# The small half of every split weight: from a VectorE subtraction to an adding transfer onto a negated tile

## The chip, the cores and the metric

The kernel runs on one core of one Trainium2 chip. The metric is device time in microseconds (us) of one launch, median of three runs; lower is better.

## The reference, cut to what matters

The reference runs a transformer of three layers over 512 tokens of width 1024, all in float32: twice (feed-forward, mixer with two kinds of attention and a short convolution, feed-forward, per-layer embedding), then once (a mixer with pooling and a recurrence, feed-forward, per-layer embedding). What the change touches is every product of an activation with a weight matrix, such as

```
def swiglu(x, w_gate, w_up, w_down):
    return (jax.nn.silu(x @ w_gate) * (x @ w_up)) @ w_down
```

The kernel makes each such product in float32 accuracy out of three products of rounded halves: with W = Wh + Wl and h = hh + hl, it adds Wh·hh, Wh·hl and Wl·hh. Wh is W rounded to the shorter type fp32r that TensorE takes, and Wl is the remainder W − Wh, rounded too.

## The kernel before, in words

Features lie on the 128 partitions, the 512 tokens along the columns. A weight is cut into units, mostly 8 row blocks of 128 by 128 columns, that is 1024 columns in memory layout. One transfer on SyncE's queue brings one unit or a few small ones into a `raw` tile (four of them, `N_RAW`). `prep` then makes the unit's tiles of up to 512 columns: for each, a pair `wh`, `wl`. In all there are 993 pairs, 937 of them 512 columns wide. `wh` is a ScalarE copy of `raw` that rounds (L136). `wl` is a VectorE subtraction `raw` − `wh` (L137); it is not issued in `prep` but noted in `self.low` and issued by `flush_low`, just before the step's product for units that the step needs itself, else just after it. A tile of 512 columns feeds 4 row blocks, and each of these feeds three products (L273 with `wh` and `hh`, L274 with `wh` and `hl`, L275 with `wl` and `hh`).

`run` walks over a list of steps (a product, an emptying of its result, a part of a norm). Each engine executes its own instructions in the order in which this walk issues them. Before each step at most one further unit is prepared while fewer than `wu` units are alive: 8 in general, 6 in the attentions, 10 at the ends of sublayers. At a boundary between sublayers a table, PLAN, sets `wu` to 0 and later to 10, so that no weight is prepared while the norm and the residual are worked out.

At a boundary, ScalarE copies the broadcast norm factor `sb` out of PSUM (L511), VectorE updates the residual x (L526, L527) and makes `hl` (L516), ScalarE makes `hh` (L528), and GpSimd sums the squares (L619 for the old sublayer, L534 for the new one) and takes the power −0.5 (L311, `s`). In the latent attention GpSimd also moves 32 rows by transfers of its own queue (L1283, 64 KB each) and makes two remainders (L1291, L1292), while VectorE scales the probabilities `p` (L1327).

Of the kernel before, what the change touches and what calls it, by code (L numbers as in the profile page):

```python
# [5 lines left out]
F32 = mybir.dt.float32  # L6
# [3 lines left out]
AF = mybir.ActivationFunctionType  # L10
ALU = mybir.AluOpType
# [3 lines left out]
T = 512  # L15
# [12 lines left out]
# What is done after each of a boundary's products: 8 half sums of the ended sublayer's last tiles (second half of  # L28
# the tokens), then 8 steps over K of the next one's first products for each half of the tokens (A, B).
# e: tile out; ss, bc: the post-norm's sum and broadcast; a, b: residual; qss, qbc: sum and broadcast of the next  # L30
# norm; w: units of weights ahead. After an embedding its 8 projections come first; p: its first gates out.
# [26 lines left out]
class Unit:  # L58
    """a weight as the tensor engine takes it: [128 rows of K, dims], from the host array host(inputs)"""
# [7 lines left out]
class Raw:  # L67
    """units that one transfer brings"""
# [17 lines left out]
class Builder:  # L86
# [31 lines left out]
    def cols_units(self, w, k0, kn, c0, ncol, width=P):  # L118
        """units of the [K, N] matrix w(inputs): rows k0*128.., columns c0..c0+ncol, a unit of `width` columns each"""

        def host(inp, c):
            a = w(inp)[k0 * P : (k0 + kn) * P, c : c + width]
            return a.reshape(kn, P, width).transpose(1, 0, 2).reshape(P, kn * width)

        return [Unit(lambda inp, c=c: host(inp, c), (kn, width)) for c in range(c0, c0 + ncol, width)]

    def prep(self, u):
        """the unit's two parts: the first on ScalarE now, the rest of it on VectorE with flush_low"""
        kn, w = u.dims
        per = T // w  # L130
        u.tiles = []
        for k in range(0, kn, per):
            n = min(per, kn - k) * w
            h, l = self.a("wh", F32R)[:, 0:n], self.a("wl", F32R)[:, 0:n]
            src = u.raw.tile[:, u.at + k * w : u.at + k * w + n]
            self.S.copy(h, src)  # L136
            self.low.append((u, lambda h=h, l=l, src=src: self.V.tensor_sub(l, src, h.bitcast(F32))))  # L137
            u.tiles.append((h, l))
        u.hi = lambda k: u.tiles[k // per][0][:, (k % per) * w : (k % per + 1) * w]
        u.lo = lambda k: u.tiles[k // per][1][:, (k % per) * w : (k % per + 1) * w]  # L140

    def declare(self, raws):
        """the transfers' sources: arrays of up to 32 MB, each transfer's part contiguous"""
        i = 0
        while i < len(raws):
            j, n = i, 0
            while j < len(raws) and (j == i or n + raws[j].n <= 32 * 2048):
                raws[j].off = n * P
                n += raws[j].n
                j += 1  # L150
            part = raws[i:j]

            def host(inp, part=part, n=n):
                out = np.empty(n * P, np.float32)
                for r in part:
                    v = out[r.off : r.off + r.n * P].reshape(P, r.n)
                    for u in r.units:
                        v[:, u.at : u.at + u.n] = u.host(inp)
                return out

            ap = self.decl(f"w{i}", (n * P,), F32, host)
            for r in part:
                r.src = ap[r.off : r.off + r.n * P].rearrange("(p n) -> p n", p=P)
            i = j

# [14 lines left out]
    def hook(self, at, fns):  # L180
        """put each of fns after the next product from step `at` on"""
        i = at
        for fn in fns:
            while not self.steps[i][2]:
                i += 1
            self.steps.insert(i + 1, ([], fn, False) + self.steps[i][3:])
            i += 2

    def run(self):
        order, last = [], {}  # L190
# [34 lines left out]
        self.low = []  # L225

        def flush_low(us=None):
            keep = []
            for u, f in self.low:
                if us is None or u in us:  # L230
                    f()
                    u.raw.left -= 1
                    if u.raw.left == 0:
                        self.rlive -= 1
                else:
                    keep.append((u, f))
            self.low[:] = keep
            load_raws()

        def prep_next():  # L240
            u = order[self.uptr]
            if u.raw.tile is None:
                flush_low()
            assert u.raw.tile is not None
            self.prep(u)
            self.uptr += 1
            self.live += 1
# [5 lines left out]
        for i, (us, fn, _, wu) in enumerate(self.steps):  # L253
            need = max([pos[id(u)] for u in us], default=-1)
            n = 0
            while self.uptr <= need or (self.uptr < len(order) and self.live < wu and n < 1):
                prep_next()
                n += 1
            lat, self.later = self.later, []
            for f in lat:  # L260
                f()
            flush_low(us)
            fn()
            flush_low()
            for u in frees.get(i, ()):
                self.live -= 1
# [10 lines left out]
    def mmk(self, o, u, h, part, cols=slice(None), start=True, stop=True, ks=None, k0=0):  # L277
        """o[cols, tokens] (+)= W[:, cols]^T h"""
        ks = list(range(u.dims[0])) if ks is None else ks
        t0, t1 = part  # L280
        for i, k in enumerate(ks):
            hh, hl = h[k0 + k]
            self.mm3(o, u.hi(k)[:, cols], u.lo(k)[:, cols], hh[:, t0:t1], hl[:, t0:t1], start and i == 0, stop and i == len(ks) - 1)

    def mm_part(self, o, p, u, h, half=None):
        """o[p] = W^T h for the tokens p, or one half of the sum over K"""
        n = u.dims[0]
# [9 lines left out]
    def sums(self, acc, part):  # L297
        """for each token of the part, tokens on partitions: the sum of acc over its rows"""
# [7 lines left out]
    def rstd(self, v, part, mul, add, dst=None):  # L306
        """(v * mul + add) ** -0.5 for each token, tokens on partitions"""
# [6 lines left out]
    def bcast(self, s, part):  # L314
        """the tokens' values s along the columns, on all partitions"""
        o = self.ps("bc")
# [16 lines left out]
    def setup_late(self):  # L333
# [5 lines left out]
        # query on partitions, key on columns: keys after the query are masked  # L339
        G.affine_select(out=m[:, 0:P], in_=m[:, 0:P], compare_op=ALU.is_ge, fill=NEG, base=0, pattern=[[-1, P]], channel_multiplier=1)  # L340
        # key on partitions, query on columns: keys from the query on are masked
        G.affine_select(out=m[:, P : 2 * P], in_=m[:, P : 2 * P], compare_op=ALU.is_gt, fill=NEG, base=0, pattern=[[1, P]], channel_multiplier=-1)
        # -1 where row >= column
# [17 lines left out]
    def columns(self):  # L361
        """the per-feature vectors, a column of 128 for each tile of features"""
# [129 lines left out]
    def boundary(self, prev, nxt):  # L492
        """The last products of prev and the first of nxt go by token halves: while one half's norm and
        residual are worked out, the tensor engine has the other half's products."""
# [96 lines left out]
    def plain_head(self, sub, units, evac, evac_at="rb"):  # L591
        """four products of h, K outermost; each half of the tokens has its half of a bank, which evac(i, p, o)
        empties: once the norm is there ("rb"), or by halves of the tokens, the second later ("halves", "both")"""
# [16 lines left out]
    def final_sq(self, sub, src, p, last, first):  # L610
        """square of a result tile into the sublayer's sum"""
# [10 lines left out]
    def ffn(self, cols, pre, post, wg, wu, uoff, wd, pieces, pmul, padd, conv=None, nxt=None):  # L622
# [18 lines left out]
        def act_gate(n, p, og):  # L641
            """the gate of hidden tile n"""
# [112 lines left out]
    def proj_sub_tail(self, sub, units, rhs, begun={}):  # L755
        """the sublayer's last product: m-tiles in T layout, squares summed; begun[m] = [o, ks]: the part of
        tile m's sum that is there already"""
# [114 lines left out]
    def mix1(self, L, cols):  # L872
# [20 lines left out]
        def heads(name, kn, h0, h1, c0, c1):  # L893
            """columns c0..c1 of heads h0..h1 of a [kn * 128, heads * n] matrix"""
# [41 lines left out]
        def rank_ss(key):  # L936
            v = self.sums(st.acc[key], FULL)
            # the rank's rms is that of r * (h W): r^2 times the raw sum of squares
# [19 lines left out]
        def rotate(src, dh, dl):  # L958
            """src [128, 512] packed heads of 32 rows: rotated, as hi/lo"""
# [132 lines left out]
        def body():  # L1092
# [70 lines left out]
            # parts of the output product (tile, k) whose operands are there before the last heads  # L1163
# [32 lines left out]
    def mix1_heads(self, sub, st, L, fn):  # L1196
        V, S, G, E = self.V, self.S, self.G, self.E
        y_rows = fn["y_rows"]
        # where a block of 512 - 128 i columns (i = 0..3) lies in three tiles
# [184 lines left out]
    def mix2(self, cols):  # L1384
# [15 lines left out]
        def gate(g):  # L1400
            """two heads of 64 a tile, on the diagonal of a [128, 128] matrix"""
# [47 lines left out]
        def lam():  # L1449
            """c8 = -8 softplus(-lambda), by feature"""  # L1450
# [375 lines left out]
def _rope_const():  # L1826
    """per row of four packed heads of 32: inverse frequency, sign of the sine"""
# [24 lines left out]
```

## Time and profile before

| what | value |
|---|---|
| median of three runs | 2894.86 us (2893.38 to 2895.28) |
| profiled execution, span from the first to the last instruction | 2893.8 us |
| TensorE busy | 2861.5 us, 99% |
| VectorE busy | 1725.2 us, 60% |
| ScalarE busy | 1256.8 us, 43% |
| GpSimd busy | 340.1 us, 12% |
| DMA, 259.29 MB on SyncE's queue | 27.7% of 16 engines |

The profiled execution has no time of its own beside its span; the median of the runs is 1.1 us above that span. Busy times of TensorE are those of pipelined products, so 99% says that it nearly always has one in flight.

### The profile page before, as it was taken

The numbers are of one execution on the slowest core, as the hardware profiler recorded it, in microseconds if no ns is written. First come the engines' busy times: TensorE is split into PE (matmuls) and PEld (weight loads), VectorE is DVE, ScalarE is ACT, GpSimd is POOL, SyncE is SP. The second block draws the span as 40 slices with busy tenths as digits, with TensorE's granted clock in tenths as the row PEclk, the third lists the DMA queues.
The fourth block names the chain that finished last, engine by engine and source line by source line (L and its number), as shares of the span: only waits on it lengthen the run. The fifth ranks groups of instructions, "written<-read, shape, count | busy, mean of one in ns | idle before, by whom it ended". The sixth has DMA issues, their size and how long they took to land.

```text
span 2893.8 us, 38786 instructions
## 1 busy us (share of the span) xinstructions
PE 2861.5 (99%) x14926; PEld 2451.1 (85%) x14928; DVE 1725.2 (60%) x3033; ACT 1256.8 (43%) x2527; POOL 340.1 (12%) x385
## 2 busy tenths in 40 slices
PE   8999999999999999999999999999999999999999
PEld 7888888898888988888888888888988889888888
DVE  6464476965434695434658773444888746635458
ACT  5332346753322363322456653323656635433234
POOL 0000130430000240000312220000320003000013
PEclk9999999999999999999999999999999999999999
DMA  5323321223223223322222223233222332322320
GB/s 177 117 92 101 102 67 48 59 74 112 99 97 108 73 74 117 102 95 95 68 76 82 65 74 116 88 103 109 78 70 91 102 102 85 111 96 95 110 95 30
DMA packets 77608, 264.31 MB, mean 91 GB/s; under 512 B 9072, under 2 KB 10992, under 8 KB 77424
## 3 DMA queue, kind: packets, MB, share of 16 engines
q1 hardware_dynamic: 75456, 259.29, 27.7%
q0 software_dynamic: 1536, 2.10, 0.3%
q8 instruction: 117, 1.92, 0.3%
q14 instruction: 67, 0.55, 0.1%
q10 hardware_dynamic: 432, 0.45, 0.0%
HBM read 257.61 MB, written 2.10 MB: 90 GB/s over the span
## 4 chain that ended last, share of the span: by engine, by line
PE 83%; DVE 11%; ACT 3%; issue 1%; POOL 1%; DMA 0%; SPq 0%; DVEq 0%; ACTq 0%; POOLq 0%
PE gu L275 13%; PE gu L274 13%; PE gu L273 13%; PE pt L275 8%; PE pt L274 8%; PE pt L273 8%; PE in L273 3%; PE in L274 3%; PE in L275 3%; DVE x L527 2%; DVE hl L516 2%; DVE t L526 2%; PE hd L274 1%; DVE wl L137 1%; PE hd L275 1%
## 5 line engine op out<-in xcount | busy, mean ns | idle before, releaser
L137 DVE TENSOR_TENSOR wl<-raw,wh 128x512 fp32r<-128x512 f32 (+1 forms) x993 | 651.2, 700 | 144.8 <-ACT wh L136 141.3
L273 PE MATMUL gu<-hh,wh 128*128 128x512 f32 x1632 | 636.5, 390 | 0.0
L275 PE MATMUL gu<-hh,wl 128*128 128x512 f32 x1632 | 635.7, 390 | 0.0
L274 PE MATMUL gu<-hl,wh 128*128 128x512 f32 x1632 | 635.7, 390 | 0.0
L136 ACT CAST wh<-raw 128x512 fp32r<-128x512 f32 (+1 forms) x993 | 543.9, 605 | 177.6 <-PE pt L274 93.7
L273 PE MATMUL pt<-dh,wh 128*128 128x512 f32 (+1 forms) x1056 | 378.1, 358 | 0.0
L275 PE MATMUL pt<-dh,wl 128*128 128x512 f32 (+1 forms) x1056 | 377.3, 357 | 0.0
L274 PE MATMUL pt<-dl,wh 128*128 128x512 f32 (+1 forms) x1056 | 377.3, 357 | 0.0
L275 PEld LDWEIGHTS gu<-hh,wl 128*128 128x128 f32 x1632 | 306.5, 188 | 63.4
L274 PEld LDWEIGHTS gu<-hl,wh 128*128 128x128 f32 x1632 | 306.5, 188 | 63.3
L273 PEld LDWEIGHTS gu<-hh,wh 128*128 128x128 f32 x1632 | 306.5, 188 | 63.1
L619 POOL TENSOR_TENSOR acc<-acc,sq 128x256 f32<-128x256 f32 (+1 forms) x96 | 98.5, 1026 | 1880.5 <-ACT sq L617 1879.6
L294 ACT CAST dh<-ur 128x512 fp32r<-128x512 f32 x112 | 69.5, 621 | 470.1 <-DVE ur L676 464.2
L670 DVE TENSOR_TENSOR ur<-gu,rb 128x512 f32<-128x512 f32 x102 | 70.5, 691 | 264.6 <-PE gu L275 264.6
L274 PEld LDWEIGHTS pt<-dl,wh 128*128 128x128 f32 x1056 | 199.7, 189 | 28.9
L273 PEld LDWEIGHTS pt<-dh,wh 128*128 128x128 f32 x1056 | 199.7, 189 | 28.8
L275 PEld LDWEIGHTS pt<-dh,wl 128*128 128x128 f32 x1056 | 199.6, 189 | 28.5
L274 PE MATMUL hd<-hl,wh 128*128 128x256 f32 (+1 forms) x672 | 203.8, 303 | 5.7 <-DVE hl L516 4.8
L273 PE MATMUL hd<-hh,wh 128*128 128x256 f32 (+1 forms) x672 | 198.7, 296 | 6.9 <-ACT hh L451 6.9
L738 DVE TENSOR_TENSOR f<-pt,f 128x512 f32<-128x512 f32 (+1 forms) x100 | 58.2, 582 | 233.2 <-PE pt L275 233.1
L275 PE MATMUL hd<-hh,wl 128*128 128x256 f32 (+1 forms) x672 | 195.1, 290 | 0.5 <-DVE wl L137 0.5
L273 PE MATMUL in<-hh,wh 128*128 128x512 f32 x432 | 170.0, 394 | 0.0
(394 smaller groups left out, 4724.4 us busy)
## 6 DMA issues: line engine op xcount, KB each, us to landing
raw<-in_w_dram SPq DMA_DIRECT2D x450, 512.0 KB, 3.5
raw<-in_w_dram SPq DMA_DIRECT2D x36, 384.0 KB, 3.1
x<-in_x_dram SPq DMA_DIRECT2D x8, 256.0 KB, 5.9
raw<-in_w_dram SPq DMA_DIRECT2D x4, 432.0 KB, 3.7
pt<-in_p_dram SPq DMA_DIRECT2D x6, 256.0 KB, 4.0
out_dram<-pgt SPq DMA_DIRECT2D x10, 128.0 KB, 1.7
qh<-qrh POOLq DMA_DIRECT2D x16, 64.0 KB, 2.0
ql<-qrl POOLq DMA_DIRECT2D x16, 64.0 KB, 2.0
```

What stands on the lines that cost most here:

```text
L136: self.S.copy(h, src)
L137: self.low.append((u, lambda h=h, l=l, src=src: self.V.tensor_sub(l, src, h.bitcast(F32))))
L273: self.E.matmul(o, lh, rh, start=start, stop=False, **kw)
L274: self.E.matmul(o, lh, rl, start=False, stop=False, **kw)
L275: self.E.matmul(o, ll, rh, start=False, stop=stop, **kw)
L294: self.S.copy(hi, src)
L516: V.scalar_tensor_tensor(hl[:, t0:t1], x, nxt.gpre(m), hh[:, t0:t1].bitcast(F32), op0=ALU.mult, op1=ALU.subtract)
L526: V.scalar_tensor_tensor(t[:, t0:t1], prev.f[m][:, t0:t1], prev.gpost(m), st.sbt[:, t0:t1], op0=ALU.mult, op1=ALU.mult)
L527: V.tensor_add(x, x, t[:, t0:t1])
L619: eng.tensor_tensor(sub.acc[:, t0:t1], sub.acc[:, t0:t1], sq[:, t0:t1], op=ALU.add)
L670: V.tensor_mul(ur[:, t0:t1], ou, sub.rb[:, t0:t1])
L738: V.tensor_tensor(f, q, f, op=ALU.add)
```

## The change

For each tile, ScalarE writes a second tile right behind the rounding copy: `wl` = −`wh`. Then a transfer on GpSimd's queue reads the same 512 columns of W from memory a second time and adds them onto `wl`. VectorE's subtraction and the list `self.low` go. A `raw` tile now counts as free when ScalarE's copies of it have been issued. Comments and docstrings went too, so that line numbers are 10 or 11 lower further down: L137 is now the copy, L138 the negation and L139 the transfer.

```diff
     def prep(self, u):
...
             src = u.raw.tile[:, u.at + k * w : u.at + k * w + n]
             self.S.copy(h, src)
-            self.low.append((u, lambda h=h, l=l, src=src: self.V.tensor_sub(l, src, h.bitcast(F32))))
+            self.S.activation(l, h.bitcast(F32), AF.Copy, scale=-1.0)
+            self.G.dma_start(l, u.raw.src[:, u.at + k * w : u.at + k * w + n], accum_op=ALU.add)
             u.tiles.append((h, l))
+            u.raw.left -= 1
+            if u.raw.left == 0:
+                self.rlive -= 1
...
-        self.low = []
-
-        def flush_low(us=None):
-            keep = []
-            for u, f in self.low:
-                if us is None or u in us:
-                    f()
-                    u.raw.left -= 1
-                    if u.raw.left == 0:
-                        self.rlive -= 1
-                else:
-                    keep.append((u, f))
-            self.low[:] = keep
-            load_raws()
...
-                flush_low()
+                load_raws()
...
-            flush_low(us)
             fn()
-            flush_low()
+            load_raws()
```

The order on ScalarE at the very start of the program, before (the first weight's two tiles, then the first normed activations `hh`):

```order
L136 CAST wh_126<-raw_102 128x512
L136 CAST wh_129<-raw_102 128x512
L451 ACTIVATE hh_132<-x_104,cols 128x512
L451 ACTIVATE hh_136<-x_105,cols 128x512
L451 ACTIVATE hh_148<-x_106,cols 128x512
```

and in the changed kernel:

```order
L137 CAST wh_126<-raw_102 128x512
L138 ACTIVATE wl_127<-wh_126 128x512
L137 CAST wh_131<-raw_102 128x512
L138 ACTIVATE wl_132<-wh_131 128x512
L440 ACTIVATE hh_136<-x_104,cols 128x512
L440 ACTIVATE hh_140<-x_105,cols 128x512
```

Two negations now stand ahead of the first `hh`.

ScalarE at the end of the first per-layer embedding, before (two units of weights, then `sb`, the broadcast norm factor that the residual waits for):

```order
L136 CAST wh_9828<-raw_9591 128x512
L136 CAST wh_9831<-raw_9591 128x512
L136 CAST wh_9863<-raw_9605 128x512
L136 CAST wh_9866<-raw_9605 128x512
L511 COPY sb_9819<-bc_9886 128x256
```

and in the changed kernel:

```order
L137 CAST wh_10194<-raw_9951 128x512
L138 ACTIVATE wl_10195<-wh_10194 128x512
L137 CAST wh_10199<-raw_9951 128x512
L138 ACTIVATE wl_10200<-wh_10199 128x512
L137 CAST wh_10231<-raw_9967 128x512
L138 ACTIVATE wl_10232<-wh_10231 128x512
L137 CAST wh_10236<-raw_9967 128x512
L138 ACTIVATE wl_10237<-wh_10236 128x512
L500 COPY sb_10185<-bc_10256 128x256
```

Four negations have come between the copies and `sb`.

GpSimd in the first latent attention, in the changed kernel (L1272 are the 64 KB moves of rows, L1280 and L1281 the remainders `kl` and `ql` of one head's operands); before, the same rows stood there without the six L139:

```order
L1272 DMA qh_4859<-qrh_4342 32x512
L1272 DMA ql_4860<-qrl_4343 32x512
L139 DMA wl_4894<-in_w_dram 128x512
L139 DMA wl_4899<-in_w_dram 128x512
L1272 DMA qh_4861<-qrh_4342 32x512
L1272 DMA ql_4862<-qrl_4343 32x512
L1280 TENSOR_TENSOR kl_4866<-kn_4782,kh_4865 64x512
L1281 TENSOR_TENSOR ql_4862<-qn_4855,qh_4861 64x512
L139 DMA wl_5006<-in_w_dram 128x512
L139 DMA wl_5011<-in_w_dram 128x512
L139 DMA wl_5042<-in_w_dram 128x512
L139 DMA wl_5047<-in_w_dram 128x512
```

The weights' transfers stand among the heads' own work on one queue. Each of them waits for its negation on ScalarE, and for the completion of the transfer eight places ahead of it on that queue.

## Rows read from the trace of the kernel before

**Rows 1.** The page: span, busy times of the engines, shares of the last-ending chain.

```profile
span 2893.8 us, 38786 instructions
PE 2861.5 (99%) x14926; PEld 2451.1 (85%) x14928; DVE 1725.2 (60%) x3033; ACT 1256.8 (43%) x2527; POOL 340.1 (12%) x385
...
PE 83%; DVE 11%; ACT 3%; issue 1%; POOL 1%; DMA 0%; SPq 0%; DVEq 0%; ACTq 0%; POOLq 0%
PE gu L275 13%; PE gu L274 13%; PE gu L273 13%; PE pt L275 8%; PE pt L274 8%; PE pt L273 8%; PE in L273 3%; PE in L274 3%; PE in L275 3%; DVE x L527 2%; DVE hl L516 2%; DVE t L526 2%; PE hd L274 1%; DVE wl L137 1%; PE hd L275 1%
```

**Rows 2.** Stretches: PE, PEld, DVE, ACT, POOL busy (instructions), clock, DMA share, GB/s.

```profile
0.00:50.00 50.00, 42.43 (x174) 33.87 (x175) 27.71 (x62) 26.81 (x45) 2.09 (x7) 1.00 0.57 193
200.00:250.00 50.00, 50.00 (x223) 41.42 (x221) 17.85 (x29) 14.03 (x25) 0.00 (x0) 1.00 0.31 97
520.00:545.00 25.00, 23.01 (x118) 18.30 (x117) 24.54 (x51) 18.40 (x46) 13.98 (x14) 0.89 0.33 101
1035.00:1085.00 50.00, 46.44 (x363) 44.02 (x361) 45.93 (x90) 31.49 (x79) 21.75 (x26) 1.00 0.17 58
2850.00:2894.00 44.00, 38.63 (x250) 34.69 (x248) 39.08 (x76) 16.89 (x37) 14.89 (x14) 0.97 0.13 48
```

**Rows 3.** Groups of instructions by line: count, busy us, mean ns, idle before.

```profile
L137 DVE TENSOR_TENSOR wl<-raw,wh 128x512 fp32r<-128x512 f32 (+1 forms) x993 | 651.2, 700 | 144.8 <-ACT wh L136 141.3
L136 ACT CAST wh<-raw 128x512 fp32r<-128x512 f32 x937 | 526.3, 617 | 177.6 <-PE pt L274 93.7 <-issue 43.2 <-DMA raw<-in_w_dram 24.3
L647 ACT ACTIVATE gr<-gr 128x512 f32<-128x512 f32 x88 | 55.2, 632 | 202.8 <-DVE gr L645 202.6
L1283 POOL DMA_DIRECT2D ql<-qrl x16 | 7.9, 491 | 0.0
L275 PE MATMUL gu<-hh,wl 128*128 128x512 f32 x1632 | 635.7, 390 | 0.0
L275 PE MATMUL pt<-dh,wl 128*128 128x512 f32 (+1 forms) x1056 | 377.3, 357 | 0.0
```

**Rows 4.** Transfers: queue q1 whole, q0 from 500 to 560 us; issues, us to landing.

```profile
q1 hardware_dynamic: 75456, 259.29, 27.7%
raw<-in_w_dram SPq DMA_DIRECT2D x450, 512.0 KB, 3.5
x<-in_x_dram SPq DMA_DIRECT2D x8, 256.0 KB, 5.9
...
q0 software_dynamic: 672, 0.92, 6.9%
ql<-qrl POOLq DMA_DIRECT2D x7, 64.0 KB, 2.3
```

**Rows 5.** Timeline of the start: start, us, engine, instruction, idle before it.

```profile
5.11 1.14 ACT L136 CAST wh<-raw 128x512 fp32r<-128x512 f32 x2 [2.65 <-DMA raw<-in_w_dram]
6.92 0.79 PE L273 MATMUL hd<-hh,wh 128*128 128x512 f32 x1 [6.92 <-ACT hh L451]
8.97 0.80 PE L275 MATMUL hd<-hh,wl 128*128 128x512 f32 x1 [0.47 <-DVE wl L137]
12.99 1.14 ACT L136 CAST wh<-raw 128x512 fp32r<-128x512 f32 x2 [2.26 <-DMA raw<-in_w_dram]
```

**Rows 6.** Timeline at the end of the first embedding, ScalarE and VectorE.

```profile
1043.58 2.21 ACT L136 CAST wh<-raw 128x512 fp32r<-128x512 f32 x4
1046.73 0.38 ACT L511 COPY sb<-bc 128x256 f32<-128x256 f32 x1 [0.95 <-PE bc L318]
...
1044.95 2.50 DVE L137 TENSOR_TENSOR wl<-raw,wh 128x512 fp32r<-128x512 f32 x4
```

**Rows 7.** Timeline in the first latent attention, GpSimd and VectorE.

```profile
538.28 1.28 POOL L1292 TENSOR_TENSOR ql<-qn,qh 64x512 fp32r<-64x512 f32 x1
...
528.12 0.48 DVE L1327 TENSOR_SCALAR p<-p,rs 128x512 f32<-128x512 f32 x1
538.35 1.50 DVE L1327 TENSOR_SCALAR p<-p,rs 128x512 f32<-128x512 f32 x1
```

## The prediction

> **What bounds the kernel now.** I read the page first. The span is 2893.8 us and TensorE is busy for 2861.5 of it; of the chain that ended last, 83% lies on TensorE, 11% on VectorE and 3% on ScalarE [rows 1]. So TensorE is the bound, and what any other engine can give back is the time in which TensorE waits: 2893.8 − 2861.5 = 32.3 us in all. The view by stretches says where that is: 7.6 us in the first 50, 5.4 in the last 44, so some 19 us in the middle, for example 2.0 in 25 us of attention and 3.6 in 50 us around the end of an embedding [rows 2]. In a feed-forward stretch there is none: 50.00 of 50 us are busy with 223 products, 0.225 us for one [rows 2]. A tile of 512 weight columns feeds 4 × 3 = 12 products, so there TensorE uses up one tile in 12 × 0.225 = **2.70 us**. Everything that is done per tile must stay under 2.70 us on its own engine, and then costs nothing there: weights are prepared up to 8 units ahead, and 7 units of two tiles are 7 × 5.4 = 38 us of cover.
>
> **The change part by part.**
>
> *Removed.* 993 subtractions, 651 us of VectorE [rows 3], which falls from 1725 to 1074 us. TensorE gains only where VectorE's queue ends a wait. `wl` of L137 has 1% of the chain [rows 1], some 29 us, and that lies mostly in places where TensorE has other work; the 19 us above are the upper bound, nothing the lower one.
>
> *Added on ScalarE.* 993 negations of an SBUF tile. None is in the trace; bounds are the copy, 0.617 us, and an activation of the same shape, 0.632 [rows 3]. I take 0.63: 993 × 0.63 = 626 us, so ScalarE goes from 1257 to 1883 us, 65%. In a feed-forward stretch it is 14.0 of 50 us [rows 2] plus 18.5 tiles × 0.63 = 11.7: no bound.
>
> *Added on GpSimd.* 993 issues. The nearest row is the issue of a 32-row transfer, 0.49 us [rows 3]. With 128 rows it costs at least that 0.49; at most four times it, 1.96, if the time goes by rows, and twice that again, 3.92, if the list of what is read doubles because the old contents are read too. The smallest end needs rows to cost nothing and the greatest needs both; I take 1.2 us, that is 44% of the 2.70, and 993 × 1.2 = 1190 us on top of GpSimd's 340.
>
> *Added on the DMA engines.* A plain load of one tile, 0.262 MB: 27.7% of 2893.8 us is 802 us of all 16 engines for 259.29 MB [rows 4], so 0.81 us a tile. GpSimd's own transfers took 6.9% of 60 us, 4.1 us, for 0.92 MB [rows 4], so 1.18 us for as many bytes, from SBUF and in rows of 2 KB. An adding transfer costs at least 0.81 (the second read hidden) and, with both reads one behind the other, 0.81 + 1.18 = 1.99. I take 1.4, about the middle. With the plain load that stays, the DMA engines then have 2.21 us of work in 2.70, against 0.81 now.
>
> The trace prices only copies. The Trainium skill, Collectives: The Full Stack, section on the bandwidth ceiling and the fold count, says that an adding transfer is limited by its two reads, which stand in one queue, so that it runs at half a copy's rate and the addition itself is free. By that rule it would be 2 × 0.81 = 1.62 us, an estimate, and the load 2.43 of 2.70; the sum stays as it is, since that still fits. No run here shows an adding transfer yet.
>
> *Moved.* A `wl` is now ready not 0.70 us after its `wh` but after 0.63 (negation) + 1.2 (issue) + landing. Landing takes 2.3 us for 64 KB from GpSimd's queue and 3.5 for 512 KB from SyncE's [rows 4]; I take 3. So 4.8 instead of 0.7: 4.1 us later. In mid-program the 38 us of cover hide that; the queue of eight outstanding transfers allows 8 × 2.70 = 21.6 us for one. Where there is no cover, it costs:
>
> - **The start.** TensorE's first product waits 6.92 us for the first `hh`, and its third product already waits for VectorE's `wl` [rows 5]. Two negations now stand ahead of the first `hh`: 2 × 0.63 = +1.3 us for the first product. The first `wl` comes at 5.11 + 0.57 + 0.63 + 1.2 + 3 = 10.5 instead of 8.97 at best, and up to 2.9 us later if its landing takes the 5.9 us of the `x` loads [rows 4], which fill the DMA engines just then. The second raw tile ends ScalarE's wait at 12.99 [rows 5] and is pushed by two adding transfers, 2 × 1.4 = 2.8. Part of this runs under other waits. I take **+5 us**, bounds +2 and +10.
> - **The ends of the two embeddings before the last.** There four casts take ScalarE from 1043.58 to 1045.79, and it then idles 0.95 us until `sb` at 1046.73 [rows 6]. Four negations add 4 × 0.63 = 2.5 us, 1.6 beyond that idle time. VectorE loses 2.5 us of subtractions in the same place [rows 6], but it then waits for `sb`. So the stall passes from VectorE to ScalarE. I take +1.5 us each, bounds −1.5 and +3: **+3 us**.
> - **The latent attentions.** In 520 to 545 VectorE is busy for 24.54 of 25 us and ScalarE for 18.40 [rows 2]. The 101 GB/s moved there are 2.5 MB, about 9 tiles beside GpSimd's own rows: VectorE loses 9 × 0.70 = 6.3 us, ScalarE gains 9 × 0.63 = 5.7, to 24.1 of 25. TensorE's waits there are 2.0 us, and since the granted clock there is 0.89 of full speed (2.4 GHz) on the mean [rows 2], another 25 × 0.11 = 2.8 us could come back. Since ScalarE is then nearly as full as VectorE was, I take −2 us for each layer. Against it, GpSimd's operands for the heads, `kl` and `ql`, stand behind up to four transfers, 4 × 1.2 = 4.8 us, part of it idle time now: +1 us. For the two layers **−2 us**, bounds −9 and +12.
>
> The other boundaries prepare no weights while the norm is worked out, and I put them at nothing: GpSimd's issues lie ahead of that work.
>
> The Trainium skill, SBUF — State Buffer, box on the "DVE blocks DMA" trap, speaks against the change: it says that GpSimd cannot write a transfer's descriptors while VectorE runs certain one-input operations that hold their shared port, so that the transfer starts late. The trace shows such holding the other way round: the scaling of `p` (L1327) took 1.50 us beside GpSimd's `ql`, and 0.48 without it [rows 7]. There are only 64 of these scalings in the program, and no other large VectorE operation of that kind outside the start, so by that rule some 9 tiles a layer are delayed by 0.5 us each, 4.5 us under 38 us of cover; it is inside the bounds of the attention.
>
> **The sum:** 5 + 3 − 2 = +6 us. On the profiled execution, 2893.8 + 6 = 2899.8; it stands 1.1 us below the median of the runs, so I predict **2901 us**, +0.2%. By the bounds: 2 − 3 − 9 = −10 to 10 + 6 + 12 = +28, 2885 to 2923.
>
> **The rivals.**
>
> *VectorE's relief pays (faster).* Of the 19 us of waits in mid-program VectorE gives back some 13, because ScalarE's extra copies fall into its idle time (it idled 0.95 us even ahead of `sb` [rows 6]); the start costs only 2. Then −11: **2884 us**. For it speaks VectorE's 24.54 of 25 us; against it, that the copies stand ahead of just the instructions that end the same waits. It decides if ScalarE's negations ahead of `sb` and in the attention add less than the idle time there.
>
> *The DMA engines become the bound (slower).* It decides at 2.70 − 0.81 = 1.89 us for an adding transfer; the upper end of the price, 1.99, is just beyond. Then a feed-forward tile takes 2.80 us, and the (1632 + 1056) / 4 = 672 feed-forward tiles [rows 3] cost 672 × 0.10 = 67 us: **2968 us**. If writing costs another 0.81, it is 672 × 0.91 = 612 us: about 3510. For it speaks that the load nearly triples and that 512 KB already take 3.5 us to land; against it, that 31% in feed-forward [rows 2] leaves two thirds free.
>
> *GpSimd becomes the bound, or late (slower).* It decides at 2.70 us for an issue. At 3.92 the 672 tiles cost 672 × 1.22 = 820 us: about 3720. At 1.96 nothing is bound in feed-forward, but in the attentions, where GpSimd has 14.0 of 25 us already [rows 2], nine transfers ask for 17.6 more, 6.6 us too many; with the same again at the heads before and after and at the norms, some 30 us: **2931 us**. For it: one queue in order, and each issue waits for ScalarE. Against it: 0.49 us for 32 rows.
>
> **How the numbers follow.** Forecast 0.55 (of it 0.06 faster by over 0.2%, 0.24 within, 0.25 slower); VectorE's relief 0.12, all faster; DMA engines 0.15; GpSimd 0.18; both slower. So faster 0.18, same 0.24, slower 0.58; 0.2%, about 6 us, is what a measurement of this kernel can tell from no change. The range goes from 2880, just under the relief's 2884, to 3100, which takes in the mild forms of both slower rivals (2931, 2968) and leaves out their hard forms and a still greater relief, under 2 in 10 together. Without the rivals it is 2885 to 2923.
>
> **What would show it.** Right: feed-forward stretches with 222 or 223 products in 50 us and no wait for `wl`; the adding transfers on queue q0 at about 1.4 us of 16 engines for a tile, near 48% of the span; 1.2 us for an issue on GpSimd; TensorE's third product at 11 to 14 us; ScalarE busy for about 1880 us, VectorE for 1070. Wrong: TensorE waiting for the landing of `wl` in feed-forward, issues above 2.7 us, `sb` not later than now, or TensorE's idle time in the middle well under 19 us.

## The result

The changed kernel takes **2966.73 us** (median of 4 runs, 2964.64 to 2970.93), the kernel before 2894.23 (4 runs in the same comparison): a ratio of **1.0251, 95% interval 1.0239 to 1.0264**, slower by 72.5 us. I had predicted 2901 with a range of 2880 to 3100. The sign and the range held; the likeliest course, with its own 2885 to 2923, did not: the time lies 44 us above it.

The page of the changed kernel, to be held against [rows 1]:

```profile
span 2965.1 us, 41294 instructions
PE 2882.1 (97%) x14928; PEld 2461.4 (83%) x14928; DVE 1133.1 (38%) x2040; ACT 1853.0 (62%) x3520; POOL 1181.4 (40%) x1378
```

VectorE lost 592 us of work, ScalarE gained 596, GpSimd 841. TensorE's idle time went from 32.3 to 2965.1 − 2882.1 = 83.0 us. Its busy time grew by 20.6 us too, though its products are the same. The first four stretches of [rows 2], with the same columns:

```profile
0.00:50.00 50.00, 36.30 (x150) 29.15 (x151) 11.65 (x35) 35.78 (x61) 20.84 (x29) 1.00 1.03 289
200.00:250.00 50.00, 50.00 (x222) 41.43 (x221) 8.90 (x13) 31.63 (x54) 20.74 (x24) 1.00 1.09 270
520.00:545.00 25.00, 22.57 (x115) 18.25 (x114) 15.55 (x32) 21.90 (x43) 14.65 (x21) 1.00 0.70 141
1035.00:1085.00 50.00, 44.51 (x340) 43.25 (x340) 26.87 (x57) 41.16 (x93) 31.51 (x38) 0.93 0.81 190
```

In the feed-forward stretch TensorE is busy for all 50 us with 222 products (223 before). (The stretches after it now hold slightly earlier work of the program.) So the time is lost at the ends and in the attentions. The groups of the work on weights (idle time at the right) and the transfers (last number: us to landing):

```profile
L139 POOL DMA_DIRECT2D wl<-in_w_dram x993 | 869.4, 900 | 1495.7 <-ACT wl L138 1198.2 <-ACT wh L137 127.8 <-DVE gr L634 25.8
L138 ACT ACTIVATE wl<-wh 128x512 fp32r<-128x512 f32 (+1 forms) x993 | 616.5, 621 | 38.3 <-PE in L263 4.8
```

```profile
q0 software_dynamic: 144528, 255.66, 49.4%
q1 hardware_dynamic: 75456, 259.29, 28.7%
...
wl<-in_w_dram POOLq DMA_DIRECT2D x937, 256.0 KB, 7.2
raw<-in_w_dram SPq DMA_DIRECT2D x450, 512.0 KB, 6.3
```

The first row is the one to read twice. GpSimd spends 869 us issuing, but 1198 us standing at a transfer whose negation ScalarE has not made yet. Whatever is queued behind that transfer stands with it. What TensorE waits for now (us in all, times, longest):

```profile
PE bc L307 <- POOL rc L300: 18.4, 11, 3.3
PE sc L262 <- DMA qh<-qrh: 16.5, 4, 6.0
PE hd L263 <- DVE hl L505: 8.8, 12, 2.1
...
PE hd L264 <- DMA wl<-in_w_dram: 5.3, 1, 5.3
PE po L262 <- ACT yph L283: 5.1, 2, 3.2
```

Before, the same list had the powers `s` and `rc` (then L311) at 3.7 us, and no wait for the moved rows `qh`:

```profile
PE bc L318 <- POOL s L311: 3.5, 8, 0.8
PE bc L318 <- POOL rc L311: 0.2, 1, 0.2
```

Now `rc` and `qh` head the list, and neither is work on a weight. At the end of the first embedding the timeline shows how it comes about (VectorE, ScalarE, GpSimd, TensorE):

```profile
1041.94 0.17 DVE L299 TENSOR_SCALAR ss<-ss 128x2 f32<-128x2 f32 x1
...
1042.66 0.63 ACT L138 ACTIVATE wl<-wh 128x512 fp32r<-128x512 f32 x1
...
1045.07 0.63 ACT L138 ACTIVATE wl<-wh 128x512 fp32r<-128x512 f32 x1
...
1042.41 0.86 POOL L139 DMA_DIRECT2D wl<-in_w_dram  x1 [0.30 <-ACT wl L138]
1043.59 0.86 POOL L139 DMA_DIRECT2D wl<-in_w_dram  x1 [0.31 <-ACT wl L138]
1044.82 0.86 POOL L139 DMA_DIRECT2D wl<-in_w_dram  x1 [0.37 <-ACT wl L138]
1045.99 0.87 POOL L139 DMA_DIRECT2D wl<-in_w_dram  x1 [0.31 <-ACT wl L138]
1046.55 1.04 POOL L300 TENSOR_TENSOR rc<-ss,mhalf 128x2 f32<-128x2 f32 x1
...
1047.64 0.69 PE L307 MATMUL bc<-ident,rc 128*128 128x128 f32 x2 [3.33 <-POOL rc L300]
```

VectorE has the sum of squares `ss` ready at 1042.11. GpSimd's power of it stands behind four transfers. These come 1.2 us apart, the pace of a copy (0.60 us) and a negation (0.63 us) on ScalarE, not of their own 0.86 us. It runs at 1046.55, and TensorE stands for 3.33 us. Afterwards its products are slower as well:

```profile
1044.00:1048.00 4.00, 0.67 (x6) 0.47 (x4) 0.55 (x2) 3.70 (x7) 2.91 (x4) 0.81 1.00 225
1048.00:1053.00 5.00, 5.00 (x25) 5.00 (x24) 2.15 (x6) 4.84 (x11) 3.04 (x4) 0.50 1.10 264
1053.00:1056.00 3.00, 3.00 (x26) 3.00 (x25) 0.42 (x1) 2.88 (x7) 2.01 (x3) 0.95 1.10 276
```

In the 5 us after the stop the granted clock is 0.50 (1.2 GHz of 2.4), with 25 products, against 26 in the following 3 us. Such stretches are the extra busy time of TensorE: over the whole run the mean granted clock went from 0.998 to 0.991, and 0.009 × 2965.1 − 0.002 × 2893.8 = 20.9 us is about the 20.6 by which its busy time grew.

At the start, to be held against [rows 5], the first and the third product:

```profile
8.37 0.80 PE L262 MATMUL hd<-hh,wh 128*128 128x512 f32 x1 [8.37 <-ACT hh L440]
...
15.28 0.80 PE L264 MATMUL hd<-hh,wl 128*128 128x512 f32 x1 [5.33 <-DMA wl<-in_w_dram]
```

In the first latent attention the same as at the embedding's end happens to the transfers of `qh`:

```profile
539.37 0.92 POOL L139 DMA_DIRECT2D wl<-in_w_dram  x1 [4.08 <-PE qn L264]
540.54 0.87 POOL L139 DMA_DIRECT2D wl<-in_w_dram  x1 [0.26 <-ACT wl L138]
541.70 0.85 POOL L139 DMA_DIRECT2D wl<-in_w_dram  x1 [0.29 <-ACT wl L138]
542.92 0.88 POOL L139 DMA_DIRECT2D wl<-in_w_dram  x1 [0.37 <-ACT wl L138]
543.46 0.86 POOL L1272 DMA_DIRECT2D qh<-qrh  x1
...
551.34 0.76 PE L262 MATMUL sc<-kh,qh 96*128 96x512 f32 x1 [5.96 <-DMA qh<-qrh]
```

Four transfers, again 1.2 us apart, stand ahead of the move of `qh`. But the move is then slow too: TensorE gets `qh` 7.9 us after the move's issue began. From 500 to 560 us the median time to landing of these 64 KB doubled (before, then changed; the adding transfers are on the same queue):

```profile
qh<-qrh POOLq DMA_DIRECT2D x7, 64.0 KB, 2.1
qh<-qrh POOLq DMA_DIRECT2D x5, 64.0 KB, 4.1
```

Both traces hold the same 14928 weight loads of TensorE in the same order. For each of them I subtracted its start in the kernel before from its start in the changed one; the table shows by how much this delay grows over stretches of the program. The last three columns are experiments that are told below. All is in us, and the stretches are given in the time of the kernel before.

| place (us of before) | changed | negations only | negations, copying transfers | copying transfers only |
|---|---|---|---|---|
| start (0 to 40) | 5.2 | 0.7 | 3.5 | 7.0 |
| inside the feed-forwards | 0.0 | 0.0 | 0.0 | 0.0 |
| latent attentions (505 to 640, 1560 to 1690) | 23.8 | 7.8 | 16.3 | −6.2 |
| ends of two embeddings (1012 to 1092, 2035 to 2150) | 25.4 | 15.9 | 23.5 | −3.5 |
| last mixer to its feed-forward (2150 to 2490) | 12.3 | 13.1 | 11.1 | −0.7 |
| other ends and begins | 3.5 | −3.1 | −0.5 | −2.9 |
| sum | 70.2 | 34.4 | 53.9 | −6.3 |

### The profile page after: what moved, and what is told of

It reads as the page before. It is cut to its first block, busy times and chain, and to the rows that moved or that the text cites. A ratio compares the mean times of both kernels' runs of the same rounds, so it can differ in the third digit from the quotient of the medians.

```text
span 2965.1 us, 41294 instructions
## 1 busy us (share of the span) xinstructions
PE 2882.1 (97%) x14928; PEld 2461.4 (83%) x14928; DVE 1133.1 (38%) x2040; ACT 1853.0 (62%) x3520; POOL 1181.4 (40%) x1378
## 3 DMA queue, kind: packets, MB, share of 16 engines
q0 software_dynamic: 144528, 255.66, 49.4%
## 5 line engine op out<-in xcount | busy, mean ns | idle before, releaser
L139 POOL DMA_DIRECT2D wl<-in_w_dram x993 | 869.4, 900 | 1495.7 <-ACT wl L138 1198.2
L137 ACT CAST wh<-raw 128x512 fp32r<-128x512 f32 (+1 forms) x993 | 592.7, 597 | 93.1 <-PE pt L263 82.2
L138 ACT ACTIVATE wl<-wh 128x512 fp32r<-128x512 f32 (+1 forms) x993 | 616.5, 621 | 38.3 <-PE in L263 4.8
L523 POOL TENSOR_TENSOR accx<-accx,sq 128x256 f32<-128x256 f32 x140 | 116.0, 828 | 158.7 <-ACT sq L522 158.7
```

Source lines behind the costliest of these rows:

```text
L138: self.S.activation(l, h.bitcast(F32), AF.Copy, scale=-1.0)
L139: self.G.dma_start(l, u.raw.src[:, u.at + k * w : u.at + k * w + n], accum_op=ALU.add)
L523: G.tensor_tensor(st.accx[:, t0:t1], st.accx[:, t0:t1], sq[:, t0:t1], op=ALU.add)
```

## The experiments

Three theories stood at the beginning: GpSimd's issue time (T1), ScalarE's added work (T2), and the two in a row, GpSimd standing at transfers for ScalarE's negations (T3). Each edit is against the changed kernel unless said; ratios are to the kernel before, whose median was 2894.5 in the first seven runs and 2893.7 to 2893.8 in the last five.

**1. The transfers go** (neg_no_transfer).

```diff
-            self.G.dma_start(l, u.raw.src[...], accum_op=ALU.add)
```

> The negations stay on ScalarE, the adding transfers go (the sum is left out: wl = -wh). Three theories for the 72.5 us. T1: GpSimd's own issue time, 0.9 us a transfer, ahead of the norms' powers and the attention's moves. T2: ScalarE's 993 negations ahead of its own copies and exponentials. T3: the two in a row: GpSimd stands at a transfer until ScalarE has come to its negation, and the power or move behind it is late though ScalarE has nothing to do with it. TensorE's waits grew by 50.7 us (32.3 to 83.0), of these 16.3 for GpSimd's powers, 16.5 for moved rows, 5.3 for the first remainders. Both T1 and T3 expect those 38 us gone and with them some of the slower products after a stop: 2905 to 2920. T2 alone expects 2950 or more.

Measured: **2927.96 us**, 1.0115 (1.0100 to 1.0130). It lies between the two expected ranges: with GpSimd free again, ScalarE's negations alone still cost 33.4 us net of VectorE's relief. `bc` now waits 2.1 us for the powers, but waits that ScalarE ends have come up, `pt` for `rb` (1.0 us in the changed kernel) and `in` for `gt` (0.3) above all:

```profile
PE pt L261 <- ACT rb L532: 9.1, 2, 4.6
...
PE in L261 <- ACT gt L1472: 3.7, 1, 3.7
PE po L261 <- ACT yph L282: 3.2, 1, 3.2
```

**2. The negations go** (copy_no_neg).

```diff
-            self.S.activation(l, h.bitcast(F32), AF.Copy, scale=-1.0)
-            self.G.dma_start(l, u.raw.src[...], accum_op=ALU.add)
+            self.G.dma_start(l, u.raw.src[...])
```

> The negations go, the transfers stay as plain copies of the same 512 columns (the remainder is left out: wl = W). GpSimd issues them without waiting for ScalarE. T1 expects most of the loss to stay, since the issues still stand ahead: 2940 to 2955. T2 and T3 expect nearly all of it gone but the start's 5 us: 2897 to 2910.

Measured: **2889.42 us**, 0.9982 (0.9973 to 0.9992). All of the loss is gone. So T1 falls, for issues of this price: 993 of them in GpSimd's queue, a second read of every weight and 4.2 us to landing cost no more than VectorE's relief gives back, if GpSimd waits for no negation. By the table 7.0 us are lost at the start and 13.3 gained in the rest, and this 13.3 is what the relief is worth at least. But these issues are cheaper than adding ones, and so are the transfers (group, then queue), so the price of adding is not tested here:

```profile
L138 POOL DMA_DIRECT2D wl<-in_w_dram x993 | 529.5, 539 | 1498.6 <-PE gu L263 620.0 <-PE pt L263 240.6 <-PE in L263 79.8
```

```profile
q0 software_dynamic: 144528, 255.66, 30.7%
```

**3. Negations and copying transfers** (neg_then_copy) tell the wait from the adding.

```diff
-            self.G.dma_start(l, u.raw.src[...], accum_op=ALU.add)
+            self.G.dma_start(l, u.raw.src[...])
```

> Everything of the change stays, only the transfer copies W over the negated tile instead of adding it (the remainder is left out: wl = W). So ScalarE's negations and GpSimd's waits for them are all there, and only the adding's own price goes: 0.87 against 0.53 us of issue, and about 7.2 against 4.2 us to the landing. The theory of the chain (ScalarE's negations alone 33.5 us, GpSimd standing at a transfer whose negation isn't made the other 39) expects 2950 to 2966. The rival, that the adding's slow issue and landing make up those 39 us, expects 2925 to 2935.

Measured: **2949.67 us**, 1.0192 (1.0178 to 1.0206), just under the lower end of the first expectation. So, put back one after the other, the parts of the 72.5 us are three: 33.4 for ScalarE's negations, 2949.7 − 2928.0 = 21.7 for the transfers that stand behind them (by the table 2.8 of it at the start), and 2966.7 − 2949.7 = 17.1 for the adding itself (0.90 instead of 0.54 us for one issue on the mean, 7.2 instead of 4.7 us to landing). Transfers without negations cost nothing net after the start in experiment 2, so what is left for the 21.7 is the standing. In another order of putting back, the parts could differ. The theory gave nearly all of the last 39 us to the standing; 17.1 of them belong to the adding. They come in part through the same two waits, which were smaller here:

```profile
PE bc L307 <- POOL rc L300: 13.9, 11, 3.0
PE sc L262 <- DMA qh<-qrh: 10.1, 3, 4.7
```

**4. VectorE negates** (neg_on_vector).

```diff
-            self.S.activation(l, h.bitcast(F32), AF.Copy, scale=-1.0)
+            self.V.tensor_scalar(l, h.bitcast(F32), -1.0, None, op0=ALU.mult)
```

> VectorE makes the negation in place of ScalarE, at once in prep; the adding transfers stay. T1: 2940 to 2955. T2: 2900 to 2910, since ScalarE is as before. T3: between, 2915 to 2935, since the transfers now wait for VectorE, which stands at products less full but at its own waits.

Measured: **2953.52 us**, 1.0201 (1.0186 to 1.0216): a miss for T2 and for T3's number. It lies just inside T1's range, but the lines show GpSimd standing, not only issuing. ScalarE is as before, and its waits at the ends are gone from the list, but GpSimd now stands 1109 us for VectorE, and the moved rows and the powers cost TensorE 22.6 + 13.5 + 2.2 = 38.3 us, against 36.5 in the changed kernel:

```profile
L139 POOL DMA_DIRECT2D wl<-in_w_dram x993 | 893.0, 1193 | 1470.1 <-DVE wl L138 1108.6 <-issue 85.9 <-PE gu L263 73.8
PE sc L262 <- DMA qh<-qrh: 22.6, 4, 6.5
PE bc L307 <- POOL rc L300: 13.5, 9, 2.4
```

By the delays of the weight loads the loss also moved: 34.4 us in the latent attentions (23.8 in the changed kernel), where VectorE was the fuller engine before [rows 2], 9.8 at the ends of the two embeddings (25.4) and 0.8 in the last mixer (12.3). So the mixer's loss goes with ScalarE's negations, and GpSimd's transfers wait for whichever engine negates.

**5. The transfers later** (lag6, lag3): issued six or three steps behind the negation.

```diff
-            self.G.dma_start(l, u.raw.src[...], accum_op=ALU.add)
...
+            self.low.append((self.at, u, lambda l=l, part=part: self.G.dma_start(l, part, accum_op=ALU.add)))
...
+                if u in us or at + 6 <= i:
+                    f()
...
```

> Copy and negation stay where they are, each adding transfer is issued six steps later than its negation (or before the step that needs it), so that GpSimd seldom finds a negation undone. Nothing is left out. T1: 2950 to 2966, since as many issues stand in the queue. T2: 2955 to 2966. T3: the waits for powers and moved rows go: 2910 to 2925; 20 us or so stay that ScalarE's own order costs.

Measured: **2982.21 us**, 1.0300 (1.0283 to 1.0317), slower still, which no theory had. The waits of T3 did go (powers 3.5 us, moved rows 2.1), but TensorE now waits for remainders that come too late, 41 us in all, for `pt` above all:

```profile
PE pt L278 <- DMA wl<-in_w_dram: 29.2, 10, 8.7
```

> As lag6, with three steps of delay in place of six. Nothing is left out. With six steps the waits for powers and moved rows were nearly gone (3.5 and 2.1 us in place of 20.0 and 16.5), but TensorE waited 43 us for remainders that came late. If both follow the delay, three steps leave some of each: 2940 to 2960, below the changed kernel's 2966.7. The rival, that any delay costs more than it gives: 2967 to 2982.

Measured: **2953.09 us**, 1.0204 (1.0189 to 1.0219), as the first of the two expected: the powers cost 3.3 us, the moved rows are not in the list, late remainders cost 6.6. Part of what is left is ScalarE's own: `pt` waits 9.3 us for `rb`, as in experiment 1. But the longest wait is a new one, 13.5 us for the sum of squares `acc` (3.9 in the changed kernel), which goes through GpSimd; which part of the delay makes it was not tested.

**6. Fewer units ahead** (paced): a unit ahead of need only at steps that hold a product.

```diff
-            while self.uptr <= need or (self.uptr < len(order) and self.live < wu and n < 1):
+            while self.uptr <= need or (mm and self.uptr < len(order) and self.live < wu and n < 1):
```

> A unit ahead of need is prepared only at steps that hold a product, not at each step, so that ScalarE gets its 2.4 us per unit of copies and negations less bunched at the ends. Nothing is left out. If the bunching is what makes ScalarE and GpSimd late: 2920 to 2945. The rival, that ScalarE simply has too much to do there: 2955 to 2980, since the units are then late themselves.

Measured: **3228.63 us**, 1.1156 (1.1141 to 1.1171), beyond both expectations. Preparing now keeps no lead, and the landing shows even in the feed-forwards (a stretch, then waits of TensorE):

```profile
200.00:250.00 50.00, 29.57 (x110) 22.94 (x109) 21.55 (x37) 14.95 (x26) 8.72 (x10) 0.76 0.48 105
```

```profile
PE gu L264 <- DMA wl<-in_w_dram: 35.8, 10, 6.3
PE pt L264 <- DMA wl<-in_w_dram: 30.7, 19, 3.2
```

It doesn't tell bunching from load, since it took the cover away as well. It does show that the transfers cost nothing in the feed-forwards only because units are prepared ahead. What the same pacing costs with the subtraction was not measured.

**7. By place** (ffn_inner, not_ffn_inner): adding transfers for the 568 inner tiles of the feed-forwards alone, then for the other 425 alone; the rest is subtracted on VectorE.

```diff
...
+        for u in gu[6:] + uu[6:]:
+            u.add = True
...
+                for u in du:
+                    u.add = True
```

> Adding transfers for the inner units of the feed-forwards alone (from the seventh tile of gate and up on, and all of down: 568 of the 993 tiles); the other units subtract on VectorE as before. Nothing is left out. If the loss is one of order at the ends and in the attentions: 2891 to 2897, no change from before, though 57% of the transfers are there. The rival, a load that counts everywhere (DMA share, GpSimd's issues): 57% of 72.5 us, 2930 to 2940.

Measured: **2895.07 us**, 1.0002 (0.9993 to 1.0011).

> The complement of ffn_inner: adding transfers for the other 425 tiles, the 568 inner ones of the feed-forwards subtract on VectorE as before. Nothing is left out. If the loss is one of order at the ends, in the attentions and in the last mixer, all of it is here: 2958 to 2970. The rival, a load that counts everywhere: 43% of 72.5 us, 2920 to 2930.

Measured: **2972.96 us**, 1.0269 (1.0253 to 1.0284). So 57% of the transfers cost nothing and the other 43% all of it, and 6 us more, whose cause is open. In ffn_inner the DMA engines are as full in a feed-forward stretch as in the changed kernel, and TensorE is busy throughout:

```profile
200.00:250.00 50.00, 50.00 (x222) 41.41 (x221) 6.92 (x10) 28.01 (x47) 20.10 (x24) 1.00 1.10 265
```

**8. The start** (start_sub): the first four units subtracted as before.

```diff
-            self.S.activation(l, h.bitcast(F32), AF.Copy, scale=-1.0)
-            self.G.dma_start(l, u.raw.src[...], accum_op=ALU.add)
+            if self.uptr >= 4:
+                self.S.activation(l, h.bitcast(F32), AF.Copy, scale=-1.0)
+                self.G.dma_start(l, u.raw.src[...], accum_op=ALU.add)
+            else:
+                self.low.append((u, lambda h=h, l=l, src=src: self.V.tensor_sub(l, src, h.bitcast(F32))))
...
```

> The changed kernel, with the first four units subtracted on VectorE as before. Nothing is left out. The start's 5.2 us go, nothing else moves: 2960 to 2963. The rival, that later waits take the time up again: 2965 to 2968.

Measured: **2961.14 us**, 1.0231 (1.0214 to 1.0249): 5.6 us less.

**9. The norm factors on VectorE** (norms_on_vector), against experiment 1.

```diff
-            S.copy(st.sbt[:, p[0] : p[1]], o[:, p[0] : p[1]])
+            V.tensor_copy(st.sbt[:, p[0] : p[1]], o[:, p[0] : p[1]])
...
-            S.copy(nxt.rb[:, p[0] : p[1]], o[:, p[0] : p[1]])
+            V.tensor_copy(nxt.rb[:, p[0] : p[1]], o[:, p[0] : p[1]])
```

> Negations on ScalarE without transfers (the sum is left out: wl = -wh; 2928.0 us so far), and at the ends VectorE copies the broadcast norm factors sb and rb out of PSUM in place of ScalarE. If ScalarE's order is what costs (these two copies stand behind three to four pairs of copy and negation there): 2914 to 2921. The rival, that the activations after them are as late: 2926 to 2931.

Measured: **2934.40 us**, 1.0139 (1.0124 to 1.0154), slower than without. The two copies alone are not what matters. The embedding's gate activation `pgt`, next on ScalarE, stands behind the same pairs, VectorE stands 6.67 us for it, and TensorE now waits 7.1 us for VectorE's part of `pgt`, a wait that experiment 1 does not have:

```profile
1044.34 0.40 ACT L830 ACTIVATE pgt<-pgt 128x256 f32<-128x256 f32 x1
...
1044.77 0.42 DVE L833 TENSOR_TENSOR prj<-prj,pgt 128x256 f32<-128x256 f32 x1 [6.67 <-ACT pgt L830]
...
PE pp L261 <- DVE pgt L829: 7.1, 2, 3.7
```

**10. The cheap parts together** (vector_lag3): VectorE negates behind the step's work, the adding transfer comes three steps later, the first four units are subtracted.

```diff
-            self.S.activation(l, h.bitcast(F32), AF.Copy, scale=-1.0)
-            self.G.dma_start(l, u.raw.src[...], accum_op=ALU.add)
...
+            else:
...
+                self.low.append((u, False, lambda h=h, l=l: self.V.tensor_scalar(l, h.bitcast(F32), -1.0, None, op0=ALU.mult)))
+                self.adds.append((self.at, u, lambda l=l, part=part: self.G.dma_start(l, part, accum_op=ALU.add)))
...
+            flush_low(us)
+            flush_adds(i, us)
             fn()
-            load_raws()
+            flush_low()
```

> The parts put together that cost least by the runs so far: VectorE makes the negation (0.44 us each) where it made the subtraction before, behind the step's own work; the adding transfer comes three steps later, so that GpSimd seldom stands at it; the first four units are subtracted. Nothing is left out. If ScalarE's negations and GpSimd's standing are the whole loss but for the adding itself: 2890 to 2905, since each alone left 54 to 60 us (VectorE's negation at once 2953.5, three steps with ScalarE's 2953.1) and the two act in one row. The rival, that the adding transfer's late landing (about 7 us) and VectorE's own queue cost by themselves: 2915 to 2940.

Measured: **2906.39 us**, 1.0039 (1.0025 to 1.0053), 1.4 us above the first expectation's upper end: 60 of the 72.5 us are gone. By the delays of the weight loads, over the stretches of the table, 11.4 us are lost at the ends of the two embeddings and 2.0 in the latent attentions, and 4.1 gained in the rest. What is left of waits that a transfer ends:

```profile
PE pt L297 <- DMA wl<-in_w_dram: 9.2, 8, 3.0
```

No version measured faster than the kernel before and computed the remainders. If the units that `pt` waits for were subtracted and the 11.4 us went with it, an estimate of 2906 − 11 = 2895 us would be left, no gain; that was not tried. Nor was an adding transfer onto a tile that no engine writes first, which would have priced the adding without any wait.

## Why the prediction was right, and where it was wrong

- **The range held by luck more than by insight.** Its upper part was there for the two slower rivals, and neither happened as described (below). The sum of the parts, with its own bounds, ended at 2923.
- **TensorE is the bound, and the feed-forwards cost nothing: right.** 222 products in 50.00 us, delays of 0.0, and ffn_inner at 1.0002.
- **Prices per tile: near.** Negation 0.62 us (0.63). Issue 869.4 / 993 = 0.88 (1.2). Adding transfer 49.4% of 2965.1 us over 993 tiles = 1.48 us of 16 engines (1.4). The copying one of experiment 2 took 30.7% of 2887.4 over 993 = 0.89, so adding costs 1.65 times a copy. The Trainium skill, Collectives: The Full Stack, section on the bandwidth ceiling and the fold count, has a factor of 2, which it states for ReduceScatter against AllGather, not for one core's transfers. The direction agrees, the factor measured here is smaller. Landing was mis-sized, 7.2 us for 3; the 38 us of cover took that up.
- **The start, +5: right.** 5.2 by the delays, 5.6 by experiment 8. The third product came at 15.28 us, later than my 11 to 14, since that transfer, issued at 6.85, took 8.4 us to land where I had 3 and 5.9 at worst. The delay is smaller than the third product's because part ran under other waits.
- **The ends of two embeddings, +3 (−3 to +6): wrong, 25.4.** The step that failed is "Four negations add 4 × 0.63 = 2.5 us, 1.6 beyond that idle time". It priced one ScalarE row, `sb`, by its idle time. The runs show three things in its place: `rc` on GpSimd, which I hadn't looked at, behind transfers that wait for ScalarE; ScalarE's own order, `pgt` and `rb` behind the same pairs by the trace (15.9 us with no transfer at all); and a granted clock of half after a stop of 3.33 us.
- **The latent attentions, −2 (−9 to +12): wrong, 23.8.** I did put GpSimd's operands behind "up to four transfers, 4 × 1.2 = 4.8 us, part of it idle time now", but counted issues. Four transfers there did stand at 1.2 us each, but that is ScalarE's pace; the same figure is luck, as an issue took 0.88. Then came the landing of the moved rows (5.96 us of wait), 4.1 us where it had been 2.1, for which I had no term. Without transfers it was 7.8 us, with copying ones 16.3. I had also weighed the rule of the Trainium skill, SBUF — State Buffer, box on the "DVE blocks DMA" trap, that GpSimd cannot write a transfer's descriptors while VectorE holds the shared port. The four issues above took 0.85 to 0.92 us and the mean of all is 0.90, so nothing of it shows here. In experiment 4, where VectorE negates, the mean issue took 1.19 us, but there the issues overlap one another (993 of them fill 893 us), so no run isolates the rule.
- **"The other boundaries prepare no weights ... and I put them at nothing": wrong.** The last mixer, for which I had no term, lost 12.3 us, all of it ScalarE's (13.1 with negations only, 0.8 with VectorE's negations): by the trace `yph` and `gt` come late. The feed-forwards' ends and begins lost 3.5.
- **VectorE's relief: inside its bounds, not in the sum.** I allowed 0 to 19 us; experiment 2 shows 13.3 at least. It is in the 72.5 already, so what was added costs more than the net says. The rival gave it 13 and was wrong that ScalarE's extra work falls into idle time.
- **DMA engines as the bound: wrong, though it named 2968.** That time came from 67 us in the feed-forwards, where nothing was lost. By the prediction's own reckoning its limit was even passed there: a DMA share of 1.09 is 1.09 × 2.70 = 2.94 us for a tile. A share above 1 means that packet times overlap, so they cannot be added up against the 2.70 us. A number that fits is no mechanism.
- **GpSimd late (2931): nearest in mechanism, wrong in reason.** Its price came from GpSimd's work, and experiment 2 shows that this work, at 0.54 us an issue, is free.

The sum as it was: 5.2 + 23.8 + 25.4 + 12.3 + 3.5 = 70.2 of the 71.3 us between the two spans. Shown by experiments are the division by cause (33.4, 21.7, 17.1, in this order of putting back) and that inner feed-forward tiles cost nothing; the finer division by place is read from the delays. Only read from the trace is which instruction of ScalarE costs how much at each end; the one attempt at it, experiment 9, moved the wait on. The 17.1 us of adding were not divided between issue and landing. ScalarE's table loads are not part of the loss: both traces hold 20 of them (ACT_TABLE_LOAD, 1.28 us each).

## What to carry to other kernels

When work is handed to an in-order queue, price it by what it waits for, not by its own duration: here an issue of 0.9 us that waited for another engine made everything behind it, related or not, as late as that engine's backlog. Before moving work off a busy engine, list for each receiving queue the few instructions that end a wait of the bounding engine, and look at what will stand ahead of each. ScalarE's average of 62% busy said nothing there; the instructions behind a burst of weight work did. Nor does taking the wait away by itself give all of it back: issued six steps later, the transfers landed too late (experiment 5).

## What was unexpected of the hardware

- An adding transfer took GpSimd 0.90 us to issue on the mean, a copying one of the same 128 rows 0.54, hardly more than the 0.49 for 32 rows [rows 3].
- The page's DMA share reached 1.09 and 1.10 in feed-forward stretches with no product late. It is a sum of packet times, and a value near 1 was no sign of a bound there. But the landing times grew (256 KB of adding transfer 7.2 us, the plain load on SyncE's queue from 3.5 to 6.3), and where nothing covers them, as for the moved rows, TensorE waited.
- A stop of 3.33 us cost TensorE more than itself: 5 us at a granted clock of 0.50 came after it.
- VectorE negated a 512-column tile in 0.45 to 0.46 us on the mean, against 0.72 for its subtraction of that shape (0.70 over all tiles [rows 3]).
